# Sliding-window extraction: one early transfer from ScalarE's queue for eight channels of sixteen batches

## The chip, the cores and the metric

The kernel runs on one core of one Trainium2 chip. The metric is device time in microseconds (us). Repeats on one chip agree within about 0.3%, so fractions of a per cent are read from five rounds in which two kernels take turns.

"Lower engines" (B in the prediction) are the eight DMA engines that carry SyncE's loads, "upper engines" (A) the other eight. A "tile" is 128 rows of 16 KB, 2 MB, stored by one scatter.

## The reference

```python
# x: 16 batches x 64 channels x 64 x 64, f32; window 8, stride 4
for i in range(15):
    for j in range(15):
        result[:, i, j] = x[:, :, 4*i : 4*i + 8, 4*j : 4*j + 8]
```

Pure data movement: 16.78 MB in, 58.98 MB of windows out (62.91 MB are counted as written).

## The kernel before

The input is kept in SBUF as `L`: partition = channel half (0 to 63 and 64 to 127), batch, band of 16 image rows; 128 KB in each. SyncE loads 28 of 32 channels of the first half by hardware-generated transfers, GpSimd the other 4 ("small") and all 32 of the second half ("big") by software-generated ones:

```python
def load(eng, ch, y, q, c0, c1):              # 8 partitions: 8 batches of one band
    p0 = ch * HP + y * QP + q
    eng.dma_start(out=L[p0 : p0 + QP - HQ + 1 : HQ, c0:c1, :, :], in_=x_v[ch, y, q, :, c0:c1, :])
...
for y in range(NY):                           # 2 groups of 8 batches
    for q in range(HQ):                       # 4 bands
        hw = y * HQ + q < HWP                 # always true here
        if hw:
            load(nc.sync, 0, y, q, SMALL, CL)           # 28 channels
        load(nc.gpsimd, 0, y, q, 0, SMALL if hw else CL)  # 4 channels
        load(nc.gpsimd, 1, y, q, 0, CL)                 # 32 channels
```

ScalarE and VectorE copy windows from `L` into one of four tiles `G`, and GpSimd scatters each full tile to HBM. The first three tiles need only y = 0. Fifteen of the 29 scatters skip every fourth row of one half (`idx_hi`: of the upper, `idx_lo`: of the lower half). The last column goes out by eight plain stores.

```python
for n in range(EARLY):       # 3 tiles of y = 0
    part(0, 2 * n)
...                          # 26 more tiles, each ended by scatter(g, index, j, s)
```

## Time and profile before

| | before |
|---|---|
| median time, 6 runs | 191.75 us |
| span of the profiled execution | 190.0 us |
| DVE / ACT busy | 142.7 / 139.2 us |
| first copies start; first scatter issued | 29.7; 44.65 us |
| last load counted complete; first scatter landed | 48.09; 52.80 us |
| 28th scatter landed | 179.11 us |

The span is a load phase (to about 48 us) and a store phase. Two quantities below come from the completion counts in the trace (no view of `prof` prints them; they were read from the packed trace). Each scatter is counted by all sixteen engines. Sorted, the counts are split into two groups of eight, the early and the late one. The **lead** is the difference of the two groups' medians; the **pace** is how far a group's median moves from one tile to the next. Paces are means over the first to ninth scatter, all of them full tiles. Which half of the engines a group is, is read from the first tile that skips rows of the upper half: the group that is short there (3.7 us instead of 4.9 to 5.0) is the upper half.

Here, the scatters' issues in the timeline (columns: start, duration, engine, line, operation; in brackets the idle time before and what ended it):

```profile
44.65 1.39 POOL L123 DMA_INDIRECT out_dram<-G,idx_y  x1 [8.49 <-ACT G L176]
46.45 2.08 POOL L123 DMA_INDIRECT out_dram<-G,idx_y  x1 [0.41 <-ACT G L176]
```

The first scatter's packets begin 2.05 us after its issue, at 46.70 us, when the loads are all but done.

### The profile page before, as it was taken

The page shows a single profiled execution, that of the slowest core. Times are in us where ns is not written, and L with a number is a line of the kernel's source. Part 1 is how long each engine was busy: PE and PEld are TensorE (multiplying, and loading weights), DVE is VectorE, ACT ScalarE, POOL GpSimd, SP SyncE. Part 2 cuts the span into 40 slices and gives each one's busy share as a digit, 9 for nine tenths or more (in the row PEclk, how much of TensorE's full clock was granted, in tenths as well). Part 3 has the DMA queues.
Part 4 walks back from the last instruction along what each step waited for, and adds up shares of the span by engine and source line. Part 5 has one row for each costly group of instructions (what it writes and reads, how often), then busy time and mean ns, then how long its engine had stood idle before and what let it go on. Part 6 is the DMA issues. An engine that isn't in the chain of part 4 may idle for free.

```text
span 190.0 us, 556 instructions
## 1 busy us (share of the span) xinstructions
DVE 142.7 (75%) x200; ACT 139.2 (73%) x89; POOL 45.7 (24%) x50
## 2 busy tenths in 40 slices
DVE  4000007999998969899989999999999999995420
ACT  0000007999999979988889889999898699993750
POOL 7402203205635321422222222222222222222000
DMA  2999999999999999999999999999999999999984
GB/s 86 319 403 402 401 399 396 403 397 396 424 438 428 412 428 428 424 410 431 438 390 436 426 414 414 438 421 407 438 410 417 423 428 414 421 438 397 435 359 169
DMA packets 11156, 75.81 MB, mean 399 GB/s; under 512 B 3456, under 2 KB 3456, under 8 KB 7552
## 3 DMA queue, kind: packets, MB, share of 16 engines
q0 software_dynamic: 9040, 66.34, 84.8%
q1 hardware_dynamic: 2048, 8.91, 12.0%
q10 hardware_dynamic: 64, 0.52, 0.7%
q14 instruction: 4, 0.03, 0.0%
HBM read 16.78 MB, written 62.91 MB: 419 GB/s over the span
## 4 chain that ended last, share of the span: by engine, by line
DMA 54%; DVE 33%; issue 6%; POOL 2%; ACT 2%; DVEq 0%; PEldq 0%; ACTq 0%
DMA L<-in_x_dram 21%; DVE G L153 17%; DMA out_dram<-G,idx_hi 13%; DMA out_dram<-G,idx_y 13%; DVE G L146 11%; DMA out_dram<-G,idx 7%; DVE G L176 4%; POOL L L58 2%; ACT G L222 2%; DVE G L143 0%; POOL pi L69 0%; DVEq L153 0%; DVEq L176 0%; PEldq L256 0%; ACTq L222 0%
## 5 line engine op out<-in xcount | busy, mean ns | idle before, releaser
L143 ACT COPY G<-L 64x2048 f32<-64x2048 f32 x46 | 87.2, 1896 | 7.6 <-DMA out_dram<-G,idx 3.9
L176 DVE COPY G<-L 32x2048 f32<-32x2048 f32 x30 | 36.7, 1224 | 29.2 <-DMA L<-in_x_dram 26.1
L153 DVE STREAM_SHUFFLE G<-L 64x1024 f32<-64x1024 f32 (+3 forms) x40 | 55.6, 1391 | 1.3
L146 DVE STREAM_SHUFFLE G<-L 64x1024 f32<-64x1024 f32 x30 | 38.4, 1282 | 0.0
L176 ACT COPY G<-L 32x2048 f32<-32x2048 f32 x18 | 33.9, 1896 | 1.4 <-DMA out_dram<-G,idx_y 0.9
L176 ACT ACT_TABLE_LOAD x1 | 1.3, 1283 | 29.7 <-DMA L<-in_x_dram 29.7
L123 POOL DMA_INDIRECT out_dram<-G,idx_y x6 | 10.9, 1812 | 25.2 <-DVE G L176 15.6
L58 POOL DMA_DIRECT2D L<-in_x_dram x16 | 10.9, 696 | 24.3 <-DMA L<-in_x_dram 23.7
L123 POOL DMA_INDIRECT out_dram<-G,idx_hi x8 | 7.7, 962 | 30.6 <-DVE G L146 19.2
L123 POOL DMA_INDIRECT out_dram<-G,idx x8 | 9.1, 1136 | 19.9 <-ACT G L157 10.6
L123 POOL DMA_INDIRECT out_dram<-G,idx_lo x7 | 6.7, 962 | 27.4 <-DVE G L146 19.0
L222 ACT COPY G<-L 32x2048 f32<-32x2048 f32 x4 | 7.6, 1896 | 4.7 <-DMA out_dram<-G,idx_lo 3.5
L157 ACT COPY G<-L 64x256 f32<-64x256 f32 (+1 forms) x20 | 9.1, 456 | 0.5
L222 DVE COPY G<-L 32x2048 f32<-32x2048 f32 x4 | 4.9, 1220 | 4.9 <-DMA out_dram<-G,idx_hi 2.5
L143 DVE COPY G<-L 64x2048 f32<-64x2048 f32 x6 | 7.3, 1222 | 0.2
L153 DVE LOAD_MASK_SELECT G<-L x40 | 0.5, 12 | 2.1 <-DMA out_dram<-G,idx_y 0.9
L72 DVE TENSOR_SCALAR tb<-pi 128x1 int32<-128x1 int32 x1 | 0.2, 153 | 1.0 <-POOL pi L69 1.0
L78 DVE TENSOR_TENSOR th<-tc,tq 128x1 int32<-128x1 int32 x2 | 0.3, 156 | 0.0
L75 DVE TENSOR_SCALAR th<-tc 128x1 int32<-128x1 int32 x2 | 0.3, 154 | 0.0
L146 DVE LOAD_MASK_SELECT G<-L x30 | 0.2, 7 | 0.0
L69 POOL IOTA pi<- 128x1 int32 x1 | 0.1, 124 | 0.4 <-PEq L256 0.4
L78 DVE CUSTOM_DVE_ANT_0 idx_lo<-idx_lo,th 128x2 uint16<-128x2 uint16 x1 | 0.2, 160 | 0.0
(18 smaller groups left out, 2.6 us busy)
## 6 DMA issues: line engine op xcount, KB each, us to landing
L<-in_x_dram POOLq DMA_DIRECT2D x8, 1024.0 KB, 21.2
L<-in_x_dram SPq DMA_DIRECT2D x8, 896.0 KB
out_dram<-G SPq DMA_DIRECT2D x6, 256.0 KB
L<-in_x_dram POOLq DMA_DIRECT2D x8, 128.0 KB, 21.4
out_dram<-G ACTq DMA_DIRECT2D x2, 256.0 KB
out_dram<-G,idx POOLq DMA_INDIRECT x8, 13.7
out_dram<-G,idx_hi POOLq DMA_INDIRECT x8, 12.3
out_dram<-G,idx_lo POOLq DMA_INDIRECT x7, 11.4
```

The source lines that it names most:

```text
L58: eng.dma_start(out=L[p0 : p0 + QP - HQ + 1 : HQ, c0:c1, :, :], in_=x_v[ch, y, q, :, c0:c1, :])
L69: nc.gpsimd.iota(pi[:, :], pattern=[[0, 1]], base=0, channel_multiplier=1)
L72: nc.vector.tensor_scalar(out=d[:, :], in0=pi[:, :], scalar1=shift, scalar2=mask, op0=ALU.logical_shift_right, op1=ALU.bitwise_and)
L75: nc.vector.tensor_scalar(out=d[:, :], in0=a[:, :], scalar1=float(m), scalar2=None, op0=ALU.mult)
L78: nc.vector.tensor_tensor(out=d[:, :], in0=a[:, :], in1=b[:, :], op=op)
L123: st = nc.gpsimd.indirect_dma_start(out=o_v, out_offset=bass.IndirectOffsetOnAxis(ap=ix[:, 0:1], axis=0), in_=g.rearrange("p c r w -> p (c ...
L143: copy(out=g[d, cs, :, :], in_=L[f, :, s * ST : s * ST + WS, cols])
L146: nc.vector.stream_shuffle(out=g[d, cs, ST:WS, :], in_=L[f, :, 0:ST, cols], mask=nxt)
L153: nc.vector.stream_shuffle(out=out, in_=in_, mask=same)
L157: act(out=out[:, 0:k], in_=in_[:, 0:k])
L176: (act if (2 * d + ch) % 3 == 0 else dve)(out=g[d * QP : (d + 1) * QP, ch * CL : (ch + 1) * CL, :, :], in_=L[f : f + QP, :, s * ST : s * S ...
L222: copy(out=g[d, ch * CL : (ch + 1) * CL, :, :], in_=L[f, :, s * ST : s * ST + WS, cols])
```

## The change

The upper engines are idle until 5.2 us. The change puts a transfer of 16 partitions, hence all engines, in front: 8 channels of one band of the second half, for all batches, from ScalarE, which has nothing to do then. GpSimd's two big loads of this band shrink from 32 to 24 channels.

```diff
+    EC = 8
+    x_b = x.rearrange("b (ch cl) (hq r) w -> ch hq b cl (r w)", ch=CH, hq=HQ)
+    nc.scalar.dma_start(out=L[HP : HP + (B - 1) * HQ + 1 : HQ, 0:EC, :, :], in_=x_b[1, 0, :, 0:EC, :])
 ...
-            load(nc.gpsimd, 1, y, q, 0, CL)
+            load(nc.gpsimd, 1, y, q, EC if q == 0 else 0, CL)
```

## The prediction

> **What bounds the kernel now.** I read the page's head first: engine shares, then the strip of forty slices and the queues.
>
> ```profile
> span 190.0 us, 556 instructions
> ...
> DVE 142.7 (75%) x200; ACT 139.2 (73%) x89; POOL 45.7 (24%) x50
> ...
> DMA  2999999999999999999999999999999999999984
> GB/s 86 319 403 402 401 399 396 403 397 396 424 438 428 412 428 428 424 410 431 438 390 436 426 414 414 438 421 407 438 410 417 423 428 414 421 438 397 435 359 169
> ...
> q0 software_dynamic: 9040, 66.34, 84.8%
> q1 hardware_dynamic: 2048, 8.91, 12.0%
> ```
>
> The DMA row is 9 from the second slice to the third from last, at about 400 GB/s while the input is loaded (to about 47 us) and 390 to 438 GB/s while tiles are stored. 16.78 MB in and 62.91 MB out is all the traffic there has to be. So the transfers bound the kernel, and the only loose time is the first slice or two and the last two. q0 is GpSimd's queue, q1 SyncE's.
>
> Second, the chain of waits in order of time, for who hands on to whom:
>
> ```profile
> 5.29 24.19 DMA L<-in_x_dram
> 29.48 0.28 issue
> 29.76 14.91 DMA L<-in_x_dram
> ...
> 46.45 11.19 DMA out_dram<-G,idx_y
> ...
> 168.34 10.77 DMA out_dram<-G,idx_hi
> ...
> 179.19 1.91 ACT G L222
> ```
>
> First loads, then stores that take 11 to 14 us each to land. A tile of 2 MB needs only about 4.85 us, so a store waits behind two others: the rings never run dry, and DVE and ACT wait for a free buffer rather than the other way round.
>
> Third, because the change acts in the first microseconds, the table by stretches (columns: width, busy time of DVE, ACT, POOL, clock, DMA share, GB/s):
>
> ```profile
> 2.00:2.25 0.25, 0.20 (x2) 0.00 (x0) 0.25 (x2) 1.00 0.00 0
> ...
> 4.00:4.25 0.25, 0.00 (x0) 0.00 (x0) 0.25 (x2) 1.00 0.51 197
> 4.25:4.50 0.25, 0.00 (x0) 0.00 (x0) 0.25 (x1) 1.00 0.53 197
> ...
> 6.00:6.50 0.50, 0.00 (x0) 0.00 (x0) 0.50 (x1) 1.00 0.97 377
> ```
>
> From 2.35 to 5.2 us the share stands at one half and the rate at 197 GB/s: eight of the sixteen DMA engines work, the other eight have nothing. The single packets confirm it: until 5.2 us all data is SyncE's, eight packets at a time. Call SyncE's eight engines B and the others A. A starts when the first 1 MB load from GpSimd has its descriptors, at 5.2 us.
>
> **What the Trainium skill says.** (1) "DMA: Bandwidth & Descriptors", section "Why a DMA increments its semaphore by 16 and not by 1": the engines used are the largest number up to 16 that divides the slowest dimension; hardware-generated transfers take the lowest-numbered ones, GpSimd's go round from a cursor. Here the old loads have 8 partitions, so 8 engines. The trace agrees: SyncE's loads complete on 8 engines; GpSimd's 4-channel loads carry their data on B, its 32-channel loads on A. The new transfer has 16 partitions, so it should use all 16. (2) Same page, "Issuing engines are not separate DMA queues": transfers share the same 16 engines, whoever issues them. So ScalarE's queue adds no bandwidth; it can only fill time in which an engine is idle. (3) Same page, "The descriptor swizzle": partitions 0 to 63 belong to engines 0 to 7, the upper ones to 8 to 15, four consecutive partitions and the four 32 above per engine. The trace agrees: in tiles that skip every fourth row of one half, eight engines write 3 rows, skip, write 3 rows. (4) "SBUF — State Buffer", section "Door 1: The DMA port swizzle": partitions 64 to 127 are reached by eight of the sixteen ports. No view of this trace shows ports; it matters for a rival below.
>
> **The change part by part.** Bytes in total are unchanged. Counted in 4 KB packets per engine:
> - Before, B has 8 SyncE transfers x 28 + 8 small ones x 4 = 256; A has 8 x 32 = 256. Evenly split.
> - Removed: 8 channels in each of two GpSimd loads, both on A: 2 x 8 = 16 packets per A engine.
> - Added: 16 partitions x 8 channels over 16 engines: 8 packets per engine, A and B alike.
> - After: A 256 - 16 + 8 = 248, B 256 + 8 = 264.
>
> Load packets follow each other every 0.16 us (A's 32-packet loads complete every 5.15 us). On A, 8 x 0.16 = 1.3 us of the new transfer falls in the idle 2.85 us, and 16 x 0.16 = 2.6 us of later work goes: A ends its loads at about 45 instead of 47.5 us. On B, busy since 2.35 us, the new packets only go between SyncE's: + 1.3 us. GpSimd's loads put one 4-byte filler packet into every engine they do not use for each data packet on the others; B loses 16 fillers at roughly 0.01 us: - 0.2 us. So B ends its loads near 49.2 instead of 48.1 us.
>
> Which half sets the end? Each tile's store needs all 16 engines. The sixteen completion counts of the last scatter fall in two groups of eight, 180.6 to 180.7 and 184.0 to 184.8 us. The group that is late is the one that does not skip rows in the first tile skipping upper partitions, so the lower-partition one; followed back packet by packet to 47 us it is, but for two crossings, SyncE's group B. B runs without a pause from 47 us on: 4.85 us a full tile, 3.65 us for a tile with three quarters of its rows. There are also 8 tiles that spare A and only 7 that spare B. So B carries the end, by over 3 us, and the change gives B 1.3 - 0.2 = 1.1 us more. ScalarE's issue itself stands in time in which ScalarE only waits; the order of every engine's computing instructions is unchanged; SyncE's eighth load and the last stores wait for other counters, all of them long since full.
>
> One gain is hidden. The first copies start when the fourth small GpSimd load has landed on B, 29.48 us. Between it and its predecessors lie the fillers of the first big load, one per SyncE packet; 8 fewer bring it about 8 x 0.16 = 1.3 us forward. ACT's chain and the first store (44.65 us) move up as much, but B then is still loading, and a store issued earlier only queues longer.
>
> Sum: 191.98 + 1.1 = 193.1 us.
>
> **The rivals.**
> 1. The idle start is filled and this is gained. Averaged over 16 engines the 256 KB hidden on A is 0.65 us: 191.3 us; were A the half that sets the end, it would be up to 2.5 us: 189.5 us. For it: the idle half is plain in the stretches, and this must be the intent. Against it: B is the late group, and gains on A only widen A's lead. My tracing of engines across 50 us is inferred from packet times, so I leave this a fifth.
> 2. The earlier first copies count: 1.3 us less, 190.7 us. Against it: stores take 11 to 14 us to land against 4.85 of work; the engines are not what is short.
> 3. The new transfer costs B more than its own packets. All its rows lie on the upper partitions, so both halves of the engines would meet at the same eight ports; B's eight packets could take twice as long and hold up SyncE's: + 2.4 us, 194.4 us. Against it: A's part is over in a few us, and B's other packets go elsewhere.
> 4. Nothing: B makes up its delay somewhere on the way (in 72 to 97 us its tiles took 4.9 to 5.1 us, so there is some slack in how fast they go): 192.0 us.
>
> **Range and chances.** Repeats differ by 0.2 us. The base case spreads over 192.6 to 193.6 us; rival 4 pulls to 192.0, rival 1 below, rival 3 up to 194.4. The range 191.8 to 194.1 leaves most of rival 1 and the extreme of rival 3 outside. Two per cent is 3.8 us; no mechanism here moves that much, 512 KB being 1.3 us of all engines. Faster 0.01, same 0.97, slower 0.02.
>
> **What would show it right or wrong.** Right: in the stretches the share rises towards 1 and the rate towards 400 GB/s soon after 2.4 us, falling back before 5 us; a third hardware queue of 0.5 MB more; the first copies near 28.2 us, first store near 43.4 us; A's last load near 45, B's near 49 us; the first store lands about a microsecond later than 52.8 us; the early group of the last scatter leads by 6 us or more, not 3.3 to 4. Wrong: a last scatter landing before 184.8 us with the groups closer together means that A was the late half; groups drifting together in mid-run means that the rings were not full; ScalarE packets of 0.3 us on B mean rival 3.

## The result, and the profile after

The changed kernel takes 190.55 us (190.44 to 190.74, six runs) against 191.75 us (191.56 to 192.25). The ratio is 0.9934, 95% interval 0.9921 to 0.9948: 1.2 us faster, and below the predicted range. A ratio here is the mean time of one kernel's fast runs over that of the other's fast runs in the same rounds, so not quite the ratio of the medians quoted.

The page of the changed kernel: strip, rates, queues.

```profile
span 189.0 us, 557 instructions
...
DMA  4999999999999999999999999999999999999993
GB/s 118 308 409 397 402 401 397 397 403 394 427 434 420 435 434 416 434 434 413 437 437 408 439 430 420 423 437 416 427 413 434 428 409 430 406 437 378 427 389 153
...
q10 hardware_dynamic: 208, 1.05, 1.8%
```

The first slice is fuller (118 against 86 GB/s) and q10, ScalarE's queue, has half a megabyte more. From the 11th to the 34th slice the rates are a little higher than before (426 against 422 GB/s on average): the store phase itself has changed, which no step of the change touches.

The first microseconds, kernel before and then changed kernel (columns: width, busy time of DVE, ACT, POOL, clock, DMA share, GB/s):

```profile
3.00:4.00 1.00, 0.54 (x4) 0.00 (x0) 1.00 (x2) 1.00 0.49 176
4.00:5.00 1.00, 0.00 (x0) 0.00 (x0) 1.00 (x3) 1.00 0.51 197
```

```profile
3.00:4.00 1.00, 0.54 (x4) 0.00 (x0) 1.00 (x2) 1.00 0.96 270
4.00:5.00 1.00, 0.00 (x0) 0.00 (x0) 1.00 (x3) 1.00 0.87 197
```

The idle half is filled as intended, but not for nothing: in the single packets SyncE's first data comes at 4.14 us instead of 2.35 us.

The seam between loads and stores of the changed kernel, from its timeline:

```profile
28.35 1.28 ACT L181 ACT_TABLE_LOAD   x1 [28.35 <-DMA L<-in_x_dram]
...
43.32 1.38 POOL L128 DMA_INDIRECT out_dram<-G,idx_y  x1 [8.49 <-DVE G L181]
45.11 2.07 POOL L128 DMA_INDIRECT out_dram<-G,idx_y  x1 [0.42 <-ACT G L181]
```

Copies and scatters start 1.33 us earlier. Yet the first scatter lands at 53.65 us, 0.85 us later than before, because the lower engines end their loads later (last load counted complete at 48.91 us instead of 48.09 us). The end was gained after that: the 28th scatter lands at 177.51 us, 1.60 us earlier.

And the store phase in two stretches, kernel before and then changed kernel (last column GB/s):

```profile
66.00:126.00 60.00, 55.49 (x82) 54.54 (x37) 13.00 (x13) 1.00 1.01 422
126.00:176.00 50.00, 46.74 (x69) 43.00 (x31) 10.59 (x11) 1.00 1.01 421
```

```profile
66.00:126.00 60.00, 56.06 (x83) 55.81 (x38) 15.42 (x13) 1.00 1.01 427
126.00:176.00 50.00, 47.52 (x69) 44.08 (x32) 11.20 (x11) 1.00 1.00 419
```

With the share at 1.00 or 1.01 in all four, the engines are as busy, but from 66 to 126 us they move 1% more (after that no more): a packet of 16 KB takes 618 ns on average (60 to 165 us) against 624 ns, where 611 ns is the undisturbed value in both traces. In the completion counts:

| | before | after |
|---|---|---|
| lead at the first scatter | 0.24 us | 2.40 us |
| pace of the early group | 4.92 us a tile | 4.94 us a tile |
| pace of the late group | 4.98 us a tile | 4.89 us a tile |
| first to 28th scatter landed | 126.3 us | 123.9 us |

So -2.4 us of store phase and +0.85 us of start. What comes after the 28th scatter is alike: the last plain store lands at 187.61 against 189.09 us (-1.5 us), and the timed runs show -1.2 us.

### The profile page after: what moved, and what is told of

It reads as the page before. It is cut to its first block, busy times and chain, and to the rows that moved or that the text cites. A ratio compares the mean times of both kernels' runs of the same rounds, so it can differ in the third digit from the quotient of the medians.

```text
span 189.0 us, 557 instructions
## 1 busy us (share of the span) xinstructions
DVE 142.5 (75%) x200; ACT 139.2 (74%) x89; POOL 46.9 (25%) x50
## 2 busy tenths in 40 slices
DMA packets 11044, 75.81 MB, mean 401 GB/s; under 512 B 3344, under 2 KB 3344, under 8 KB 7440
## 3 DMA queue, kind: packets, MB, share of 16 engines
HBM read 16.78 MB, written 62.91 MB: 422 GB/s over the span
## 4 chain that ended last, share of the span: by engine, by line
DMA 66%; DVE 18%; issue 6%; ACT 3%; POOL 2%; DVEq 0%; ACTq 0%; PEldq 0%
DMA out_dram<-G,idx_hi 24%; DMA L<-in_x_dram 23%; DMA out_dram<-G,idx 13%; DVE G L158 10%; DMA out_dram<-G,idx_y 7%; DVE G L151 5%; DVE G L181 3%; ACT G L227 2%; POOL L L58 2%; ACT G L148 1%; DVE G L148 0%; DVEq L181 0%; POOL pi L69 0%; DVEq L158 0%; PEldq L261 0%
## 5 line engine op out<-in xcount | busy, mean ns | idle before, releaser
L128 POOL DMA_INDIRECT out_dram<-G,idx_y x6 | 10.0, 1664 | 25.5 <-DVE G L181 24.5
L128 POOL DMA_INDIRECT out_dram<-G,idx x8 | 11.3, 1412 | 19.9 <-DVE G L158 6.5
```

The costliest lines, as they stand in the source:

```text
L128: st = nc.gpsimd.indirect_dma_start(out=o_v, out_offset=bass.IndirectOffsetOnAxis(ap=ix[:, 0:1], axis=0), in_=g.rearrange("p c r w -> p (c ...
```

## The experiments

Four theories were to be told apart:
- **GAP**: the filled idle time is the gain.
- **GATE**: the earlier first copies are.
- **LEAD**: the upper engines go ahead and then disturb the lower ones less.
- **The recorded one**: only bytes on the lower engines count.

From the second batch on there was also **BUNCH**: engines that waited for the first scatter start in step and stay slow.

All 15 runs gave correct results; times are from five rounds, medians, ratios against the kernel before on the same chip. The other columns come from the profiled execution of each.

| run | 1st scatter issued | landed | lead then | late group, us a tile | 28th landed | 1st to 28th | time, us | ratio |
|---|---|---|---|---|---|---|---|---|
| before | 44.65 | 52.80 | 0.24 | 4.98 | 179.11 | 126.3 | 191.75 | |
| changed | 43.32 | 53.65 | 2.40 | 4.89 | 177.51 | 123.9 | 190.55 | 0.9934 |
| e1_late | 45.89 | 55.00 | 0.31 | 4.99 | 181.45 | 126.5 | 194.50 | 1.0141 |
| e2_even | 44.11 | 52.10 | 0.34 | 4.98 | 178.30 | 126.2 | 191.89 | 1.0012 |
| e3_lower | 44.40 | 52.97 | 1.02 | 4.89 | 178.79 | 125.8 | 191.86 | 1.0011 |
| e4_gate | 40.67 | 53.00 | 0.47 | 4.86 | 176.62 | 123.6 | 189.11 | 0.9866 |
| e5_moreB | 44.47 | 57.14 | 1.03 | 4.87 | 180.72 | 123.6 | 194.06 | 1.0123 |
| e6_hold | 44.50 | 53.51 | 0.42 | 4.98 | 180.19 | 126.7 | 193.13 | 1.0074 |
| e7_ec4 | 44.06 | 53.17 | 0.85 | 4.91 | 178.37 | 125.2 | 191.48 | 0.9998 |
| e8_ec16 | 44.34 | 55.38 | 3.53 | 4.87 | 179.56 | 124.2 | 192.38 | 1.0034 |
| e9_third | 43.28 | 53.55 | 2.53 | 4.88 | 177.78 | 124.2 | 190.51 | 0.9933 |
| e10_level | 43.85 | 55.38 | 2.40 | 4.85 | 179.16 | 123.8 | 191.95 | 1.0012 |
| e11_stagger | 44.82 | 52.97 | 0.23 | 4.99 | 179.24 | 126.3 | 192.21 | 1.0023 |
| e12_shift | 44.83 | 53.22 | 0.54 | 4.93 | 179.31 | 126.1 | 192.26 | 1.0026 |
| e13_lead | 44.65 | 54.39 | 1.67 | 4.88 | 178.95 | 124.6 | 191.75 | 1.0000 |
| e15_best | 40.72 | 53.17 | 1.96 | 4.85 | 175.58 | 122.4 | 188.54 | 0.9843 |
| e16_gate13 | 43.88 | 52.99 | 0.37 | 4.95 | 179.20 | 126.2 | 191.62 | 0.9996 |

The stretch from the first to the 28th scatter takes 125.8 to 126.7 us or 122.4 to 124.6 us, with only e7_ec4 between.

### e1_late: without the idle time

```diff
-    nc.scalar.dma_start(out=L[HP : ...], in_=x_b[1, 0, :, 0:EC, :])        # at the start
+    nc.vector.tensor_copy(out=L[HP : HP + 1, 0:1, 0:1, 0:8], in_=L[0:1, 0:1, 0:1, 0:8])
+    nc.scalar.dma_start(out=L[HP : ...], in_=x_b[1, 0, :, 0:EC, :])        # after the loads
```

> The changed kernel, but ScalarE's transfer is issued only when the first small load has landed (about 9 us), so the idle 2.85 us of the upper engines is not filled; bytes per engine are those of the changed kernel. LEAD (the upper engines finish their loads some us ahead, and the two halves then disturb each other less in the store phase): most of the gain stays, ratio to before 0.993 to 0.996. GAP (the gain is the filled idle time): the gain is gone, 1.000 or above. GATE (the first copies start 1.3 us earlier): the fillers are fewer as in the change, gain stays, 0.993. My recorded theory (the lower engines' bytes set the end) would have 1.005.

It took 194.50 us, worse than any theory said. The transfer ran from 12.8 to 17.1 us in the midst of the others and delayed the first scatter to 45.89 us. The upper engines then had nothing to do before it came, the lead was 0.31 us and the pace 4.99. GAP's forecast (1.000 or above) came true, but the gate and the end of the loads had moved as well: a confounded run that decides nothing.

### e4_gate: an earlier gate, the same bytes

```diff
-            if hw:
-                load(nc.sync, 0, y, q, SMALL, CL)
-            load(nc.gpsimd, 0, y, q, 0, SMALL if hw else CL)
+            if q < HQ - 1:
+                load(nc.sync, 0, y, q, SMALL, CL)
+                load(nc.gpsimd, 0, y, q, 0, SMALL)
+            else:
+                load(nc.sync, 0, y, q, 0 if y == 0 else 2 * SMALL, CL)
+                load(nc.gpsimd, 0, 1, q, y * SMALL, (y + 1) * SMALL)
```

> The kernel before, but the last small load that the first copies wait for goes to SyncE's queue and another of the same size takes its place; bytes per engine unchanged, no transfer from ScalarE. First copies should start near 26 us instead of 29.7, the first store near 41 us instead of 44.7. GATE: faster by 1.3 us or more, ratio 0.993 or below. LEAD and GAP: 1.000 within 0.002, since neither the split of bytes nor the idle start changes.

189.11 us, ratio 0.9866. LEAD and GAP, as then put, are refuted for this kernel: no byte changed engines. But it was not the head start as such. Its timeline:

```profile
25.70 1.28 ACT L179 ACT_TABLE_LOAD   x1 [25.70 <-DMA L<-in_x_dram]
...
40.67 1.56 POOL L126 DMA_INDIRECT out_dram<-G,idx_y  x1 [4.57 <-ACT G L179]
```

The first scatter is issued 4 us earlier, and lands 0.2 us later than before: its packets begin at 46.70 us, as in the kernel before, behind the loads. The gain is the pace, 4.86 us a tile in both groups (126.3 to 123.6 us). The lead is only 0.47 us, and it is none of one half over the other: in the first tile that skips upper rows the groups take 4.05 and 4.47 us, so the sixteen engines of both halves are mixed, spread over 1.0 us. So a tile can be fast without a lead of one half.

Why an earlier queued scatter has this effect was not isolated. In the kernel before, too, the stretches at the seam show hardly any idle engines that it could have filled, the share from 47 to 48 us (0.91) being the lowest:

```profile
45.00:46.00 1.00, 0.97 (x2) 1.00 (x1) 1.00 (x1) 1.00 1.13 374
46.00:47.00 1.00, 1.00 (x1) 1.00 (x2) 0.59 (x2) 1.00 1.28 431
47.00:48.00 1.00, 0.99 (x2) 0.96 (x1) 1.00 (x1) 1.00 0.91 369
```

### e5_moreB: more bytes for the lower engines

```diff
+    for n in range(2):          # into G[3], not yet in use
+        nc.sync.dma_start(out=g3[32 * n : 32 * n + 8], in_=x_v[0, n, 0, :, 0:4, :])   # g3: G[3] in 4 parts
```

> The kernel before with two more loads of 128 KB at the end of SyncE's loads, into a buffer not yet in use: 8 packets, 1.3 us, more on each lower engine, nothing else changed. LEAD: the upper half starts the stores 1.3 us ahead, so the lower half gains speed and the end moves by less than 1.3 us or even earlier, ratio 0.996 to 1.002. GAP, GATE and my recorded theory: later by 1.3 us, ratio 1.007.

194.06 us. The edit did more than intended: each of its two loads wrote to eight neighbouring partitions, which by the Trainium skill's "SBUF — State Buffer", section "Door 1: The DMA port swizzle", reach two ports. In this trace the rate was down to 107 to 115 GB/s from 46 to 49 us, about a quarter of the usual one; the first scatter landed 4.3 us late. As a test of the end it failed. Still, the pace after it was 4.87, and the 28th scatter of the profiled run, the fastest of its five with 193.55 us, only 1.6 us late.

### e6_hold: the change with the old gate

```diff
+    act(out=G[3][0:32, 0:23, :, :], in_=L[0:32, 0:23, 0:WS, 0:WS])
+    dve(out=G[3][32:64, 0:32, :, :], in_=L[0:32, 0:32, 0:WS, 0:WS])
     for n in range(EARLY):
         part(0, 2 * n)
```

> The changed kernel with one more copy of about 1.3 us on ScalarE and VectorE each ahead of the first copies, which puts their start and the first store back to where they were before the change (first store near 44.7 us). GATE: the gain is gone, ratio 1.000. LEAD and GAP: the gain stays, 0.993 to 0.995.

193.13 us, ratio 1.0074: the whole gain is gone and more. The stretches at the seam, changed kernel and then this one:

```profile
45.00:46.00 1.00, 0.99 (x2) 1.00 (x1) 0.89 (x1) 1.00 1.05 430
46.00:47.00 1.00, 1.00 (x1) 0.63 (x1) 1.00 (x1) 1.00 1.01 382
```

```profile
45.00:46.00 1.00, 0.97 (x2) 1.00 (x2) 1.00 (x1) 1.00 0.51 209
46.00:47.00 1.00, 0.99 (x2) 1.00 (x2) 0.95 (x1) 1.00 0.52 197
```

In the changed kernel the first upper engines go over to stores at 45.3 us, after a short wait (the DMA share from 44 to 45 us is 0.94). Here they stand idle for two to three microseconds, until the first scatter's packets come at 47.57 us; the lower engines have by then caught up, the lead is 0.42 us, and the pace 4.98. With this, the split of bytes costs what the prediction said (first scatter 0.7 us late) and gives nothing back.

### e9_third: only the third scatter later

```diff
     for n in range(EARLY):
+        if n == EARLY - 1:
+            act(out=G[3][0:32, 0:26, :, :], in_=L[HP : HP + 32, 0:26, 0:WS, 0:WS])
         part(0, 2 * n)
```

> The changed kernel with one more copy of 1.5 us on ScalarE just ahead of its last copy into the third tile: the third store is issued after the loads have ended (about 49.4 us instead of 47.8), the first two as in the changed kernel. BUNCH (a half of the engines that has to wait for the first store starts it in step and then needs 4.93 to 5.0 us a tile instead of 4.85): nothing changes at the first store, lower half stays at 4.86 us a tile, ratio 0.993 to 0.997. If what matters is that three stores are queued before the loads end: the gain is gone, 1.000 or above.

190.51 us, ratio 0.9933, as the change. The third scatter was issued at 48.59 us (47.82 in the changed kernel), less late than aimed at but after the loads' last packet, which ends at 48.14. So it does not matter whether the third scatter is queued before the loads end. The second was issued at 45.08 us, as in the changed kernel (45.11); a later second one was not tested.

### e10_level: meant to remove the lead

```diff
+    nc.gpsimd.dma_start(out=g3[0:8, 0:1, :], in_=x_v[0, 0, 0, :, 0:1, :])      # on e4_gate
+    nc.gpsimd.dma_start(out=g3[32:40, 0:4, :], in_=x_v[1, 0, 0, :, 0:4, :])
```

> The earlier-gate kernel with 0.64 us of needless loads more on the upper engines and 0.16 us on the lower ones, so that both halves end their loads together; the first stores are queued long before. BUNCH: no engine waits for a store, both halves stay near 4.85 us a tile, time that of the earlier-gate kernel plus 0.2 to 0.7 us, 189.3 to 189.9 us. LEAD (what counts is that one half is ahead): both halves in step, the rate falls, 191.5 us or more.

191.95 us, but not for the reason given: the additional transfers held up GpSimd's own issues (first scatter at 43.85 instead of 40.67 us), the first landing was 2.4 us later, and the lead was 2.4 us, not zero. The pace was 4.85. It failed as a test of the level start and is one more case of a large lead with a fast late group.

### e11_stagger and e12_shift: four or eight lower engines later

```diff
+    nc.sync.dma_start(out=g3[0 : 4 * n - 3 : 4], in_=x_v[0, 0, 0, 0:n, 0:4, :])   # n = 4 (e11), 8 (e12)
```

> The kernel before with a needless load of 4 packets (0.64 us) at the end of SyncE's queue on four of the eight lower engines alone. BUNCH: these four start the stores out of step with the others, the lower half's tiles cost about 4.86 us instead of 5.0, and the end comes 1 to 2 us earlier although the kernel moves more bytes. If only bytes count: later by 0.3 to 0.64 us.

> The kernel before with the same needless 4 packets on all eight lower engines. BUNCH: the lower half now ends its loads after the first store has been queued and goes over to it engine by engine; first store 0.6 us later, tiles near 4.86 us, end 1 to 2 us earlier. LEAD: the same. If only bytes count: later by 0.64 us, ratio 1.003.

192.21 and 192.26 us. Delaying four engines of the late group did not speed it up (4.99 us a tile). It is a weak test of BUNCH: the counts of the lower engines' last small load spread over 1.17 us instead of 0.83, so they were hardly more out of step than before. With all eight 0.64 us later the lead was 0.54 us; the late group ran at 4.84 to 4.89 us for five tiles, came up to the early group, which does 4.92, and then fell to 5.0, which BUNCH did not expect. In the end the bytes were paid for. The run e8_ec16 below speaks more clearly against BUNCH for the late group: there its eight counts of the first scatter lie within 0.22 us (0.48 us in the kernel before), so it starts in step, and it runs at 4.87.

### e13_lead: three times as many needless bytes

```diff
+    for n in range(3):
+        nc.sync.dma_start(out=g3[n : n + 29 : 4], in_=x_v[0, 0, 0, :, 0:4, :])
```

> The kernel before with three needless loads of 4 packets each (1.9 us) on all eight lower engines at the end of SyncE's queue; first copies and first store as before. If LEAD holds (with the upper half about 2 us ahead the lower half needs 4.86 us a tile instead of 5.0, some 2.4 us less to the end): the first store lands near 54.6 us instead of 52.8, but the end is no later than with one such load, 191.2 to 192.3 us. If only bytes count: 193.7 us or more, ratio 1.010.

191.75 us, ratio 1.0000 (0.9985 to 1.0016). 1.9 us more of loads than the kernel before, all on the half that sets the end, and no later; 1.3 us more of loads than e12_shift, and half a microsecond earlier. The first scatter landed 1.6 us late, the store phase took 1.7 us less. Its stretch from 66 to 126 us, then that of e12_shift:

```profile
66.00:126.00 60.00, 55.87 (x81) 55.71 (x38) 15.05 (x13) 1.00 1.01 427
```

```profile
66.00:126.00 60.00, 55.60 (x82) 54.67 (x37) 14.14 (x13) 1.00 1.01 422
```

Gate, first copies and idle start are those of the kernel before; what differs is the needless bytes and the lead that they make (1.67 us). This shows that a lead of the upper half makes the lower half faster. That the lower engines now find a scatter queued cannot be the reason alone: it holds for e12_shift too.

### e2_even and e3_lower: the idle start with another split

```diff
-    EC = 8                                                     # e2_even
+    EC = 4
+    nc.scalar.dma_start(out=L[0 : (B - 1) * HQ + 1 : HQ, SMALL : SMALL + EC, :, :], in_=x_b[0, 0, :, SMALL : SMALL + EC, :])
-                load(nc.sync, 0, y, q, SMALL, CL)
+                load(nc.sync, 0, y, q, SMALL + EC if q == 0 else SMALL, CL)
```

e3_lower takes all 8 channels from the lower half in the same way and leaves GpSimd's loads whole.

> ScalarE loads 4 channels of each half early, so that both halves of the engines load as many bytes as in the kernel before and the idle start of the upper half is still used. First store issued near 44 us. LEAD: the upper half ends its loads 1.3 us earlier and goes ahead, the lower half ends as before; first store lands near 52.9 us, lower half near 4.86 us a tile, 189.3 to 190.2 us, so faster than the change. If the early gate alone mattered: between the kernel before and the change, 191.0.

> The change mirrored: the 8 channels come from the lower half, out of SyncE's loads. Lower engines 248 packets, upper 264 of which 8 in the idle start; the small loads, and with them the gate, move little. LEAD: the halves end within 1 us of each other and wait for the first store together, slow tiles (5.0 us), 191.0 to 192.0 us. If bytes on the lower half set the end: earlier by about 1.3 us, 190.4 us.

191.89 and 191.86 us, no gain in either. e2_even uses the idle start and its first scatter lands 0.7 us earlier than before; the halves end their loads together (lead 0.34 us), the pace is 4.98, and the profiled run, the fastest of its five at 191.19 us, has the 28th scatter 0.8 us earlier. My forecast of a lead was wrong. GAP is refuted as the cause of the gain: the gap is filled here too, and nothing is gained. In e3_lower the early group ran at 4.97 us a tile until the late one reached it, then the late one fell to 5.0.

### e16_gate13, e7_ec4 and e8_ec16: which part is needed, and how much

```diff
+    for n in range(2):                                         # e16_gate13, on e4_gate
+        act(out=G[3][0:32, 23 * n : 23 * n + 23, :, :], in_=L[0:32, 0:23, 0:WS, 0:WS])
+        dve(out=G[3][32:64, 32 * n : 32 * n + 32, :, :], in_=L[0:32, 0:32, 0:WS, 0:WS])
-    EC = 8                                                     # e7_ec4: 4, e8_ec16: 16, on the change
```

> The earlier-gate kernel with 2.7 us of extra copies ahead of the first ones, so that the first store is issued about where the changed kernel issues it (43.4 us) while the bytes per engine are those of the kernel before and ScalarE loads nothing: the gate part of the change alone. If the queued first store alone is what keeps the tiles fast: both halves near 4.85 us a tile, 189.1 to 189.6 us. If the lead from the split of bytes is needed as well: slow tiles, 191.3 us or more.

> The change with 4 channels instead of 8: first store issued near 44 us, lower engines 260 packets, upper 252. LEAD: the upper half is about 1 us ahead at the first store; first landing near 53.3 us, lower half near 4.87 us a tile, 190.2 to 190.8 us. If 1 us of lead is too little: 191.5 us or more.

> The change with 16 channels: lower engines 272 packets, upper 240. LEAD: the upper half leads by 3 us or more, tiles stay at 4.86 us, but the lower half starts its stores 1.3 us later than with 8 channels: 191.5 to 192.2 us. If more early load is better in itself: below 190.0 us.

e16_gate13 has the gate of the change alone, nearly (43.88 against 43.32 us): lead 0.37 us, pace 4.95, 191.62 us, nothing gained. e6_hold had the split alone: nothing gained. Neither part at the size that it has in the change gains anything alone; the change needs both. With 4 channels (191.48 us) the lead of 0.85 us shrank to 0.61 us in five tiles, with the late group at 4.86 to 4.88 us, which then fell to 5.0: 125.2 us from first to 28th scatter, between the two groups of runs. With 16 channels (192.38 us) it lasted nearly to the end, but the lower engines began 1.7 us later than with 8.

### e15_best: both, for the half that sets the end

e4_gate, with ScalarE's 8 early channels taken from the lower half as in e3_lower.

```diff
+    nc.scalar.dma_start(out=L[0 : (B - 1) * HQ + 1 : HQ, SMALL : SMALL + EC, :, :], in_=x_b[0, 0, :, SMALL : SMALL + EC, :])
-                load(nc.sync, 0, y, q, SMALL, CL)
+                load(nc.sync, 0, y, q, SMALL + EC if q == 0 else SMALL, CL)      # q < 3
```

> The earlier-gate kernel with ScalarE's early load of 8 channels taken from the lower half: early first stores (near 40 us), fewer packets on the half that sets the end (248 against 264). Expected: first store lands near 52.3 us, tiles near 4.86 us, 188.3 to 189.1 us, as fast as the earlier-gate kernel or faster. If a lead of the upper half is needed: slow tiles, 190.5 us or more.

188.54 us, ratio 0.9843 (0.9828 to 0.9857): faster than both kernels. The groups are 1.96 us apart, with the lower half ahead now (in the first tile that skips upper rows it is the late group that is short), and it is the lower half that has more rows to store. Both groups run at 4.85 to 4.86 us a tile. The stretch from 66 to 126 us:

```profile
66.00:126.00 60.00, 56.84 (x84) 57.04 (x38) 15.79 (x14) 1.00 1.01 431
```

## Why the prediction was wrong

**Right, step by step.**
- Idle upper engines until 5.2 us, filled by the transfer: shown by the stretches.
- First copies near 28.2 us and first scatter near 43.4 us: measured 28.35 and 43.32.
- Upper loads end near 45 us: the eight upper engines count the last one complete between 45.03 and 46.49 us, so this held for the first of them. Lower loads end near 49.2 us: 48.91.
- The first scatter lands about a microsecond later: 0.85 us.
- The lower half, with more rows, sets the end: in the last scatter of the changed kernel the late group still trails by 2.6 us.

**A size off.** The transfer put SyncE's first data back by 1.8 us, where eight packets were counted as 1.3. From 4.1 to 5 us, where packets of both queues run, those of 4 KB took about 315 ns instead of 159. This is the sign that the prediction gave for rival 3. ScalarE's transfer, to upper partitions alone, ran on sixteen engines at 171 GB/s from its first packet to its last, less than the 197 GB/s of SyncE's eight before; that fits the ports of rival 3, but its cause was not isolated. The net delay of 0.85 us is nevertheless near the 1.1 us forecast. (The 62.91 MB out that the prediction takes for traffic include the skipped rows; all queues together moved 75.81 MB, loads included.)

**The step that failed** is "B runs without a pause from 47 us on: 4.85 us a full tile", and with it that the 1.1 us would go through to the end. 4.85 us was the best interval, not the mean. Before the change the late group needed 4.98 us a tile over the first nine, and the engines were busy all the while: the loss lay within the packets (624 against 611 ns), where neither the busy row nor the chain of waits shows it. The change made it 4.89. I had seen tiles of 4.9 to 5.1 us and read them, in rival 4, as slack to make up for a delay; they were a cost that a small shift of the start could remove.

**The sign that was misread.** The prediction said that more lead for the upper half would be useless, and that its lead at the end would grow to 6 us or more. It shrank, from 3.65 to 2.6 us. The lead was useful for the other half: e13_lead gets it from needless bytes alone, and the gain pays for them in full. Two of the signs of being wrong came true, but not their readings. The last scatter landed before 184.8 us (183.2) with the groups closer, yet the upper half was the early one, being short in the first tile that skips upper rows (3.71 against 4.86 us). The groups drifted together in mid-run (2.40 us at the first scatter, 1.62 at the 17th), yet the engines did not run out of work: the DMA share stays at 1.00 to 1.01.

**The rivals.** Rival 1 (filled time gained) falls with e2_even. Rival 2 (earlier copies) named a number, 190.7 us, close to the measured one, by luck: e16_gate13 has almost the same gate and no gain. In the change the earlier gate matters because upper engines that end their loads from 45 us on find a scatter in the queue and hardly wait, so that they keep their lead (e6_hold). Rival 4 named the place but not the size.

**What stays open.** Shown: in the kernel before and the five runs where the halves land the first scatter within 0.42 us of each other, the late half needs 4.95 to 4.99 us a tile; in the six kernels with a lead of 1.67 us or more it runs at 4.85 to 4.89, for about half of the store phase or longer, while the lead shrinks by less than 0.1 us a tile. Between these, leads of 0.54 to 1.03 us, it is one or the other for some tiles (4.87 to 4.93 on average). A lead of one half of 1.67 us or more is enough, but it is not the only way: e4_gate is fast with mixed engines and 0.47 us.

Not shown: what the two groups contend for; why e4_gate is fast; why a slowed group stays slow when the lead has grown again to 1.5 us and more; why the early group does 4.85 to 4.86 in e4_gate, e5_moreB and e15_best but 4.92 to 4.97 in most others. How far its eight counts lie apart does not tell: 0.34 to 0.61 us in those three, 0.13 in the kernel before, but 0.77 in the changed one. In most kernels the late group needs 4.95 us or more after about 145 us; this is not explained. e10_level, which was to set the lead to zero with early scatters, failed.

## What to carry to other kernels

Where all DMA engines are busy, measure their pace, tile by tile and half by half, before calling it a limit: here 1 to 2% lay in packets of 16 KB that took 624 ns instead of 611. In this kernel, queueing the first store 4 us earlier brought 2.5 us (e4_gate, cause open), and together with an earlier start for the half that has more to store 3.1 us (e15_best), against 1.2 us of the change. A change that touches the start of a saturated stream can gain or lose by the order in which its engines come out of it, so test each part alone.

## What the Trainium skill lacked or had wrong

- "DMA: Bandwidth & Descriptors": nothing on two groups of engines that store side by side and slow each other. Here the late half needs 4.95 to 4.99 us a tile when it lands the first scatter within 0.42 us of the other, 4.85 to 4.89 us when 1.67 to 3.53 us apart (2 MB tiles of 16 KB rows).
- The same page, section "Queues, rings and completion order", says that an engine turns from one queue to the next after a packet of typically 9 to 17 descriptors. In this trace GpSimd's and SyncE's descriptors alternate about one by one on the lower engines, a 4-byte one and then a 4 KB one: of those that start from 14 to 18 us in the kernel before, 206 are of 4 bytes and 175 of SyncE's 4 KB. Packets here may hold a single descriptor each; the trace does not tell.
- The same page, on how many engines a transfer uses, does not say that a GpSimd transfer on eight engines also puts one 4-byte descriptor per data packet on the other eight. Behind SyncE's packets that delays completion: in the kernel before, the first big load is counted by the upper engines at 11.2 to 11.6 us and by the lower ones at 13.6 to 14.4 us.
- The same page says that queues take turns. ScalarE's and SyncE's transfers were both issued at 0.74 us, and SyncE's first data came only at 4.14 us, when most of ScalarE's was through; with four channels in place of eight at 3.05 us, with sixteen at 5.70 us. Whether the engines or the making of descriptors held SyncE's back, the trace does not show. No page has this.
